# Two transformer blocks on one core: re-ordering a finished instruction list so that TensorE stays with one kind of product

## The chip, the cores and the metric

One NeuronCore of a Trainium2 chip. The metric is the device time of one execution in microseconds (us); lower is better. TensorE is called PE here, VectorE DVE, ScalarE ACT, GpSimd POOL; SP issues the DMAs.

## The reference

Both blocks work on 256 tokens of width 1024, in fp32, and each has two layers.

```python
def first_block(x, c, ...):                      # twice
    shift1, scale1, gate1, shift2, scale2, gate2 = split(silu(c) @ w_ada[l] + b_ada[l], 6)
    hdn = modulate(rmsnorm(x, norm1_g[l]), shift1, scale1)
    q_lat, c_kv, k_pe, sb_qkv, mb_qkv, gates = split(hdn @ w_in[l])     # 1024 -> 7200
    o_mla = causal_softmax_attention(...)        # latents of 768 and 256, normed, then w_uq, w_ukv
    o_sb  = stick_breaking_attention(...)
    o_mb  = moba_attention(...)
    g_a, g_b, g_c = split(sigmoid(gates), 3)
    merged = g_a*(o_mla @ w_o_mla[l]) + g_b*(o_sb @ w_o_sb[l]) + g_c*(o_mb @ w_o_moba[l])
    x = x + gate1 * (merged @ w_out[l])
    hdn = modulate(rmsnorm(x, norm2_g[l]), shift2, scale2)
    x = x + gate2 * (square(relu(hdn @ w_ff1[l])) @ w_ff2[l])           # 1024 -> 4096 -> 1024

def second_block(x, c, ctx, c_ctx, ...):         # _layer twice, the context only in the first
    h, hc = normed and modulated x and context
    parts = split(h @ w_in)                      # the context's parts likewise
    o_att = silu(z) * attention(rope(q), [k_context; rope(k)], [v_context; v])
    o_f = silu(z) * (real(fftn(u)) @ w_fourier)
    o_c, o_p = convolution and pooling branches
    x = x + gate * (concat(o_f, o_att, o_c, o_p) @ w_out)
```

## The kernel before

The program is not written in the order in which it runs. `record` (line 493) describes the whole computation once, as a list of operations for five queues: PE, DVE, ACT, POOL and SP. `Recorder.add` (line 230) finds for each operation which others it depends on. `Scheduler.run` (line 425) then simulates the list with a table of costs and sets a start time for each operation; `emit` (line 434) sorts the list by that time (line 451) and writes each instruction at line 454, which is why every row of the trace says L454. On the chip every engine goes through its own queue in that order and waits at its head until what the instruction needs is there. So the order decides who waits.

The scheduler is a list scheduler. `forward` (line 341) takes the operation with the smallest priority whose predecessors are placed and whose buffers are free, and puts it into the first gap of its engine that is long enough. `backward` (line 406) works out how late each could start, and that becomes the priority of the next of five passes, less an offset from the table `LEAD` (line 1792), which has numbers for each part of the model, with or without an engine. Buffers come from pools (`SLOTS`, `CAPS`, lines 1788, 1789): at most 24 split weight tiles and 8 raw ones at once. Two things are not in the scheduler's costs: that PE may take longer after a change of the kind of product, and which PE work could fill a wait.

A weight tile (`wload`, line 596) is brought by a DMA (`raw`), rounded to fp32r on ACT (`whi`), and the remainder is made on DVE (`wlo`). A large product (`mm3`, line 523) is three fp32r matmuls: high by high, high by low, low by high. On PE there are three kinds of instructions: 6920 fp32r products, 538 transposes of 128x128 blocks, and 412 plain fp32 products (scores, probabilities by values, row sums).

The names that the rows use: `g`, `gc`, `ff`, `f`, `cb`, `qkvp`, `ufp` are PSUM tiles of the large products; `nT_ql`, `nT_kvl`, `nT_x`, `nT_c` are transposes of normed rows (`norm_T`, line 782: the latents for queries and keys in the first block, x and the context in the second; the number behind the name is layer and token half); `xn_...` are those rows, made on DVE; `s_ml`, `s_l` are score tiles, `p_...` their softmax (DVE and ACT), `pT_...` its transposes on PE, and `pv` the product with the values; `gh`, `yt`, `of` are the three steps of the Fourier branch, with copies between them.

```python
    with tc.manual_schedule():
        for op in sorted(rec.ops, key=lambda o: (o.start, o.idx)):
```

Of the kernel before, what the change touches and what calls it, by code (L numbers as in the profile page):

```python
# [14 lines left out]
F32 = mybir.dt.float32  # L15
# [3 lines left out]
ALU = mybir.AluOpType  # L19
# [11 lines left out]
PSUM_CLASSES = ("mm", "tr")  # L31
# [112 lines left out]

class Op:
    __slots__ = ("idx", "eng", "fn", "args", "kw", "cost", "preds", "succs", "bufs", "start", "end", "inst", "lead",
                 "calls")

    def __init__(self, idx, eng, fn, args, kw):
        self.idx, self.eng, self.fn, self.args, self.kw = idx, eng, fn, args, kw  # L150
# [17 lines left out]
class Recorder:  # L168
# [61 lines left out]
    def add(self, eng, fn, args, kw):  # L230
        if self.group:
            op = self.group[0]
        else:
            op = Op(len(self.ops), eng, fn, args, kw)
            op.lead = 0.0 if eng == "sync" else sum(
                LEAD.get(q, 0.0) for q in (self.part, self.stage, f"{self.stage}/{eng}"))
            self.ops.append(op)
# [83 lines left out]
class Scheduler:  # L321
# [84 lines left out]
    def backward(self):  # L406
# [15 lines left out]
            late[op.idx] = total - r - op.cost  # L422
        return late

    def run(self, passes):

        prio = list(range(len(self.ops)))
        for i in range(passes):
            if i > 0:
                prio = [t - op.lead for t, op in zip(self.backward(), self.ops)]  # L430
            self.forward(prio)


def emit(tc, ctx, rec):
    nc = tc.nc
    sb = ctx.enter_context(tc.tile_pool(name="sb", bufs=1))
    ps = ctx.enter_context(tc.tile_pool(name="ps", bufs=1, space=bass.MemoryType.PSUM))
    dr = ctx.enter_context(tc.tile_pool(name="dr", bufs=1, space=bass.MemoryType.DRAM))

    def val(x):  # L440
        if not isinstance(x, View):
            return x
        b = x.buf
        if b.real is None:
            pool = ps if b.cls in PSUM_CLASSES else dr if b.cls == "dram" else sb
            tag = b.name if b.slot is None else f"{b.cls}_{b.slot}"
            b.real = pool.tile(list(b.shape), b.dtype, tag=tag, name=b.name)
        return x.resolve()

    with tc.manual_schedule():  # L450
        for op in sorted(rec.ops, key=lambda o: (o.start, o.idx)):
            op.inst = []
            for fn, args, kw in op.calls:
                op.inst.append(getattr(getattr(nc, op.eng), fn)(*[val(x) for x in args],  # L454
                                                                 **{k: val(x) for k, x in kw.items()}))
# [37 lines left out]
def record(nc, a, out):  # L493
# [570 lines left out]
    def lead_first(g, act, banks):  # L1064
# [85 lines left out]
        first_weights.extend(last)  # L1150
        rate[0] = RATE

# [629 lines left out]
    for l in range(L):  # L1782
# [5 lines left out]
SLOTS = {"s4": 40, "s2": 11, "sm": 40, "mm": 4, "tr": 4}  # L1788
CAPS = {"w": 24, "r": 8}
PASSES = 5  # L1790
RATE = 0.4386
LEAD = {"None/sync": -6220.0, "None/tensor": -670.0, "None/vector": -290.0, "ada/sync": 8040.0, "att mb0": -60.0,
# [16 lines left out]
        "lead": 3119.0, "lead weights": 2070.0, "mb": -1510.0, "ml": -12100.0, "norm": 2550.0, "out mb0": -2320.0,  # L1809
# [22 lines left out]


@with_exitstack
def kernel(ctx: ExitStack, tc: tile.TileContext, a: dict, out: bass.AP):
    rec = Recorder()
    record(rec, a, out)
    Scheduler(rec, SLOTS, CAPS).run(PASSES)
    emit(tc, ctx, rec)
# [33 lines left out]
```

## Time and profile before

| what | value |
|---|---|
| median of 3 runs | 1278.47 us (1277.05 to 1279.66) |
| the profiled execution's own time | 1279.97 us |
| its span in the trace | 1278.2 us |
| PE busy | 1255.5 us, 98% |
| weight loads busy (beside PE) | 1112.8 us, 87% |
| DVE busy | 1043.1 us, 82% |
| ACT busy | 726.0 us, 57% |
| POOL busy | 85.2 us, 7% |
| DMA queue of the data | 62.9% of 16 engines' span |

The sums are made against the profiled execution: its span is 1278.2 us, and its own time is 1.8 us longer. Matmuls are pipelined, so a row's own duration on PE (0.39 us for one of 512 columns) overlaps the next one; the distance between the starts of two rows is what a product costs in a queue that never waits. A row with x4 is four equal instructions in succession.

### The profile page before, as it was taken

The page shows a single profiled execution, that of the slowest core. Times are in us where ns is not written, and L with a number is a line of the kernel's source. Part 1 is how long each engine was busy: PE and PEld are TensorE (multiplying, and loading weights), DVE is VectorE, ACT ScalarE, POOL GpSimd, SP SyncE. Part 2 cuts the span into 40 slices and gives each one's busy share as a digit, 9 for nine tenths or more (in the row PEclk, how much of TensorE's full clock was granted, in tenths as well). Part 3 has the DMA queues.
Part 4 walks back from the last instruction along what each step waited for, and adds up shares of the span by engine and source line. Part 5 has one row for each costly group of instructions (what it writes and reads, how often), then busy time and mean ns, then how long its engine had stood idle before and what let it go on. Part 6 is the DMA issues. An engine that isn't in the chain of part 4 may idle for free.

```text
span 1278.2 us, 22019 instructions
## 1 busy us (share of the span) xinstructions
PE 1255.5 (98%) x8282; PEld 1112.8 (87%) x8282; DVE 1043.1 (82%) x1707; ACT 726.0 (57%) x1247; POOL 85.2 (7%) x112
## 2 busy tenths in 40 slices
PE   6999999999999999999999999999999999999998
PEld 4899989998898989999889988899888777787997
DVE  4989989986876668798888879988878769958885
ACT  6597767554654546667576555555655353426561
POOL 1000000210000000000001200000002021100310
PEclk9999999999999999999999999999999999999999
DMA  8967665865997758576666766788652416716530
GB/s 295 367 236 240 210 224 202 280 199 191 315 300 275 253 165 276 182 246 200 233 205 198 266 231 228 269 275 279 210 190 79 156 31 215 238 34 213 175 119 33
DMA packets 164336, 272.68 MB, mean 213 GB/s; under 512 B 26411, under 2 KB 57343, under 8 KB 164230
## 3 DMA queue, kind: packets, MB, share of 16 engines
q1 hardware_dynamic: 164230, 271.28, 62.9%
q8 instruction: 65, 1.06, 0.3%
q14 instruction: 41, 0.34, 0.1%
HBM read 270.11 MB, written 1.13 MB: 212 GB/s over the span
## 4 chain that ended last, share of the span: by engine, by line
PE 88%; DMA 4%; DVE 3%; issue 2%; ACT 1%; SPq 1%; POOL 0%; ACTq 0%; POOLq 0%
PE gc L454 17%; PE g L454 16%; PE f L454 14%; PE ff L454 13%; PE cb L454 11%; PE qkvp L454 3%; DMA wraw_l<-lead_w 2%; PE ufp L454 1%; DMA araw_l<-lead_ada 1%; PE rs L454 1%; PE end L454 1%; DMA raw<-w_in 1%; PE pv L454 1%; PE s_l L454 1%; PE pT_l L454 1%
## 5 line engine op out<-in xcount | busy, mean ns | idle before, releaser
L454 DVE TENSOR_TENSOR wlo<-raw,whi 128x1024 fp32r<-128x1024 f32 (+2 forms) x354 | 407.8, 1184 | 57.5 <-ACT whi L454 32.6
L454 ACT CAST whi<-raw 128x1024 fp32r<-128x1024 f32 (+3 forms) x354 | 349.6, 1014 | 170.3 <-PE ff L454 43.2
L454 DVE SCALAR_TENSOR_TENSOR acc<-araw,cT,acc 128x1024 f32<-128x1024 f32 x147 | 191.9, 1330 | 1.3 <-DMA araw<-w_mod 0.6
L454 PE MATMUL gc<-hT1h,whi 128*128 128x256 f32 x256 | 73.9, 289 | 0.0
L454 PE MATMUL gc<-hT1h,wlo 128*128 128x256 f32 x256 | 71.8, 281 | 0.0
L454 PE MATMUL gc<-hT1l,whi 128*128 128x256 f32 x256 | 71.6, 280 | 0.0
L454 PE MATMUL f<-fT1h,whi 128*128 128x256 f32 x192 | 54.2, 282 | 0.0
L454 PE MATMUL f<-fT0h,whi 128*128 128x256 f32 x192 | 53.9, 281 | 0.0
L454 PE MATMUL f<-fT1h,wlo 128*128 128x256 f32 x192 | 53.9, 281 | 0.0
L454 PE MATMUL f<-fT1l,whi 128*128 128x256 f32 x192 | 53.9, 281 | 0.0
L454 PE MATMUL f<-fT0l,whi 128*128 128x256 f32 x192 | 53.8, 280 | 0.0
L454 PE MATMUL f<-fT0h,wlo 128*128 128x256 f32 x192 | 53.8, 280 | 0.0
L454 PE MATMUL cb<-h20h,whi 128*128 128x512 f32 x128 | 53.2, 416 | 0.0
L454 PE MATMUL gc<-hT0h,whi 128*128 128x256 f32 x176 | 51.5, 293 | 0.0
L454 PE MATMUL cb<-h20h,wlo 128*128 128x512 f32 x128 | 50.5, 394 | 0.0
L454 PE MATMUL cb<-h20l,whi 128*128 128x512 f32 x128 | 50.4, 394 | 0.0
L454 PEld LDWEIGHTS gc<-hT1h,whi 128*128 128x128 f32 x256 | 48.3, 189 | 1.8 <-issue 1.1
L454 PE MATMUL gc<-hT0l,whi 128*128 128x256 f32 x176 | 49.4, 281 | 0.0
L454 PE MATMUL gc<-hT0h,wlo 128*128 128x256 f32 x176 | 49.3, 280 | 0.0
L454 PEld LDWEIGHTS gc<-hT1l,whi 128*128 128x128 f32 x256 | 48.2, 188 | 0.6
L454 PEld LDWEIGHTS gc<-hT1h,wlo 128*128 128x128 f32 x256 | 48.2, 188 | 0.0
L454 PE MATMUL g<-whi,hT1h 128*128 128x512 f32 (+1 forms) x112 | 42.6, 380 | 0.0
(651 smaller groups left out, 3826.0 us busy)
## 6 DMA issues: line engine op xcount, KB each, us to landing
raw<-w_ff SPq DMA_DIRECT2D x128, 512.0 KB
raw<-w_in SPq DMA_DIRECT2D x126, 512.0 KB
araw<-w_ada SPq DMA_DIRECT2D x96, 256.0 KB
araw<-w_ada SPq DMA_DIRECT2D x32, 512.0 KB
raw<-w_out SPq DMA_DIRECT2D x32, 512.0 KB
araw<-w_mod SPq DMA_DIRECT2D x64, 256.0 KB
raw<-w_in SPq DMA_DIRECT2D x24, 352.0 KB
araw_l<-lead_ada SPq DMA_DIRECT2D x32, 256.0 KB
```

The costliest lines, as they stand in the source:

```text
L454: op.inst.append(getattr(getattr(nc, op.eng), fn)(*[val(x) for x in args], **{k: val(x) for k, x in kw.items()}))
```

## The change

No instruction is added or removed, but for one more loading of an ACT table (10 in place of 9). Two things are new. First, a function `settle` is called at the end of `run`. It takes the schedule that the five passes left, keeps the order on DVE, ACT, POOL and SP and the buffers, and runs the whole list once more in order of time with other costs: `span` for the durations, `HAND` for the time from one engine to the next, and `TURN` for what PE is to pay when one kind of product follows another (kind 0 fp32r, 1 transposes, 2 and 3 fp32 with a wide or a narrow result). Whenever PE's next operation is not ready, or is a large product while PE is at another kind, it looks up to 4 us (`LOOK`) further down the list and takes a ready one, of the same sort if there is one, for at most 1.5 us of work in succession (`MOST`). The order it finds is what `emit` writes. Second, the table `LEAD` has new numbers, so the schedule that `settle` starts from is another.

```diff
+    HAND = {"tensor": 200.0, "vector": 150.0, "scalar": 150.0, "gpsimd": 100.0}
+    TURN = ((0.0, 0.0, 60.0, 92.0), (84.0, 0.0, 0.0, 92.0), (188.0, 0.0, 0.0, 100.0), (239.0, 135.0, 135.0, 0.0))
...
+    def settle(self, look, most):
...
+            q = queue["tensor"]
+            while taken[q[head["tensor"]]]:
+                head["tensor"] += 1
+            h = head["tensor"]
+            first, now = q[h], free["tensor"]
+            late = left[first] > 0 or ready(first) > now + 100.0
+            i = first
+            if last is not None and (late or last[0] and not form[first][0]) and ahead < most:
+                other = None
+                for j in range(h + 1, len(q)):
+                    c = q[j]
+                    if ops[c].start > ops[first].start + look:
+                        break
+                    if taken[c] or left[c] or ready(c) > now + 60.0:
+                        continue
+                    if bool(form[c][0]) == bool(last[0]):
+                        other = c
+                        break
+                    if late and other is None:
+                        other = c
+                if other is not None:
+                    i = other
...
+            ahead = 0.0 if i == first else ahead + span[i]
+            t = max(now, ready(i))
...
+            elif form[i][0] != last[0]:
+                t += self.TURN[last[0]][form[i][0]]
...
     def run(self, passes):
...
+        self.settle(LOOK, MOST)
...
-        for op in sorted(rec.ops, key=lambda o: (o.start, o.idx)):
+        for op in sorted(rec.ops, key=lambda o: o.seq):
...
+LOOK, MOST = 4000.0, 1500.0
...
-LEAD = {"None/sync": -6220.0, "None/tensor": -670.0, "None/vector": -290.0, "ada/sync": 8040.0, "att mb0": -60.0,
+LEAD = {"None/scalar": 2080.0, "None/sync": -5820.0, "None/tensor": -670.0, "None/vector": -290.0,
```

Counted over PE's whole queue, there are 164 stretches of transposes before and 98 after, 36 stretches of wide fp32 products and then 28, and 42 of narrow ones in both. The places where the order differs that matter below are three; all are on PE.

**At the boundary of the second block's two layers**, where the context's normed rows `xn_c` are transposed. `qkvp` is the projection of x to queries, keys and values of layer 1. Before, six of its products stand ahead of `nT_c12`:

```order
L454 MATMUL qkvp10_12938<-whi182_0_12591,h21h0_12809 128x512
L454 MATMUL qkvp10_12938<-wlo182_0_12636,h21h0_12809 128x512
L454 MATMUL qkvp10_12938<-whi182_0_12591,h21l0_12828 128x512
L454 MATMUL qkvp10_12938<-whi182_0_12591,h21h0_12809 128x512
L454 MATMUL qkvp10_12938<-wlo182_0_12636,h21h0_12809 128x512
L454 MATMUL qkvp10_12938<-whi182_0_12591,h21l0_12828 128x512
L454 MATMUL nT_c120_12960<-ct_79,xn_c12_12953 128x128 x4
L454 MATMUL nT_c124_12965<-ct_79,xn_c12_12953 128x128 x4
L454 MATMUL qkvp10_12938<-whi182_2_12604,h21h1_12817 128x512
```

Now twelve stand there (ten of them shown); the six more are products that came behind the transposes before:

```order
L634 MATMUL qkvp10_12961<-whi182_0_12566,h21l0_12821 128x512
L634 MATMUL qkvp10_12961<-whi182_0_12566,h21h0_12810 128x512
L634 MATMUL qkvp10_12961<-wlo182_0_12618,h21h0_12810 128x512
L634 MATMUL qkvp10_12961<-whi182_0_12566,h21l0_12821 128x512
L634 MATMUL qkvp10_12961<-whi182_2_12614,h21h1_12814 128x512
L634 MATMUL qkvp10_12961<-wlo182_2_12620,h21h1_12814 128x512
L634 MATMUL qkvp10_12961<-whi182_2_12614,h21l1_12825 128x512
L634 MATMUL qkvp10_12961<-whi182_2_12614,h21h1_12814 128x512
L634 MATMUL qkvp10_12961<-wlo182_2_12620,h21h1_12814 128x512
L634 MATMUL qkvp10_12961<-whi182_2_12614,h21l1_12825 128x512
L634 MATMUL nT_c120_12974<-ct_79,xn_c12_12956 128x128 x4
L634 MATMUL nT_c124_12985<-ct_79,xn_c12_12956 128x128 x4
```

In the same way there are 12 products ahead of the second half's `nT_c` in place of 3 that had nothing of it to wait for, and three more `g` products ahead of `nT_x11`.

**In the first layer, at the transposes of the key latents** `nT_kvl01`. `g8` is the up-projection of the query latents and `s_sb` a score of the stick-breaking attention. Before, the transposes follow those of the query latents at once:

```order
L454 MATMUL g8_00_1216<-whi8_2_946,laT0l0_1207 128x384
L454 MATMUL nT_ql010_1249<-ct_79,xn_ql01_1242 128x128 x4
L454 MATMUL nT_ql014_1256<-ct_79,xn_ql01_1242 128x128 x2
L454 MATMUL nT_kvl010_1261<-ct_79,xn_kvl01_1225 128x128 x2
L454 MATMUL g8_00_1216<-whi9_0_1005,laT0h1_1205 128x384
L454 MATMUL g8_00_1216<-wlo9_0_1066,laT0h1_1205 128x384
L454 MATMUL g8_00_1216<-whi9_0_1005,laT0l1_1220 128x384
```

Now six `g8` products, which stood behind them or ahead of `nT_ql01`, and a score stand between:

```order
L634 MATMUL nT_ql010_1246<-ct_79,xn_ql01_1207 128x128 x4
L634 MATMUL nT_ql014_1257<-ct_79,xn_ql01_1207 128x128 x2
L634 MATMUL g8_00_1236<-whi8_2_956,laT0h0_1178 128x384
L634 MATMUL g8_00_1236<-wlo8_2_961,laT0h0_1178 128x384
L634 MATMUL g8_00_1236<-whi8_2_956,laT0l0_1194 128x384
L634 MATMUL g8_00_1236<-whi9_0_1000,laT0h1_1192 128x384
L634 MATMUL g8_00_1236<-wlo9_0_1005,laT0h1_1192 128x384
L634 MATMUL g8_00_1236<-whi9_0_1000,laT0l1_1199 128x384
L634 MATMUL s_sb011_1274<-kssb01_805,qssb01_776 128x256
L634 MATMUL nT_kvl010_1276<-ct_79,xn_kvl01_1202 128x128 x2
L634 MATMUL s_sb011_1274<-k_low1_75,qssb01_776 128x256
```

**At the end of attention in the last layer**, where `pT_l1101`, transposes of softmaxed scores, are followed by the products with the values. `cb` is the product with the columns of the convolution and pooling branches. Before, three of its four transposes stand further up, each alone, and the last one here:

```order
L454 MATMUL cb1_1792_0_13872<-h21l3_12842,whi191_4_13667 128x256
L454 MATMUL cb1_1792_0_13872<-h21h3_12833,wlo191_4_13858 128x256
L454 MATMUL cb1_1792_1_13890<-h21h3_12833,whi191_4_13667 128x256
L454 MATMUL cb1_1792_1_13890<-h21l3_12842,whi191_4_13667 128x256
L454 MATMUL cb1_1792_1_13890<-h21h3_12833,wlo191_4_13858 128x256
L454 MATMUL pT_l1101_14070<-ct_79,p_l1101_14019 128x128
L454 MATMUL pv2101_14072<-pTs_l1001_13999,qkv10_13027 64x128
L454 MATMUL pv2101_14072<-pTs_l1011_14064,qkv10_13027 64x128
```

Now three groups of four stand together, and `pv` follows:

```order
L634 MATMUL cb1_1536_0_13950<-h21l1_12825,whi190_0_13412 128x256
L634 MATMUL cb1_1536_0_13950<-h21h1_12814,wlo190_0_13717 128x256
L634 MATMUL cb1_1536_1_13954<-h21h1_12814,whi190_0_13412 128x256
L634 MATMUL cb1_1536_1_13954<-h21l1_12825,whi190_0_13412 128x256
L634 MATMUL cb1_1536_1_13954<-h21h1_12814,wlo190_0_13717 128x256
L634 MATMUL pT_l1011_13976<-ct_79,p_l1011_13848 128x128 x4
L634 MATMUL pT_l1101_13993<-ct_79,p_l1101_13940 128x128 x4
L634 MATMUL pT_l1111_14000<-ct_79,p_l1111_13894 128x128 x4
L634 MATMUL pv2101_14015<-pTs_l1001_13929,qkv10_13064 64x128
```

Between the second score product of this softmax, `s_l1101`, and its transposes stand now 24 `cb` products and one group of transposes.

## Rows read from the trace of the kernel before

**Rows 1.** The page: busy time by engine; granted clock of PE in 40 slices, in tenths.

```profile
PE 1255.5 (98%) x8282; PEld 1112.8 (87%) x8282; DVE 1043.1 (82%) x1707; ACT 726.0 (57%) x1247; POOL 85.2 (7%) x112
...
PEclk9999999999999999999999999999999999999999
```

**Rows 2.** Windows: us, then PE, PEld, DVE, ACT, POOL busy, clock, DMA.

```profile
9.00:70.00 61.00, 56.37 (x380) 48.46 (x381) 48.63 (x99) 36.57 (x57) 0.56 (x1) 1.00 0.97 343
70.00:1000.00 930.00, 928.44 (x6273) 839.97 (x6272) 778.71 (x1188) 558.78 (x933) 42.60 (x52) 1.00 0.68 229
...
1170.00:1195.00 25.00, 25.00 (x199) 24.38 (x198) 23.69 (x55) 14.28 (x25) 5.13 (x4) 1.00 0.62 200
```

**Rows 3.** Timeline of PE at a lone transpose (start us, duration us, instruction).

```profile
653.89 0.28 PE L454 MATMUL gc<-hT1h,wlo 128*128 128x256 f32 x1
654.02 0.27 PE L454 MATMUL pT_ml<-ct,p_ml 128*128 128x128 f32 x1
...
654.25 0.28 PE L454 MATMUL gc<-hT1l,whi 128*128 128x256 f32 x1
654.37 0.28 PE L454 MATMUL gc<-hT1h,wlo 128*128 128x256 f32 x1
```

**Rows 4.** Timeline of PE: plain fp32 scores; one product behind each is left out.

```profile
188.85 1.03 PE L454 MATMUL s_ml<-mkT,mqT 96*128 96x256 f32 x4
...
189.95 0.39 PE L454 MATMUL g<-wlo,hT0h 128*128 128x512 f32 x1
...
622.85 0.61 PE L454 MATMUL s_ml<-mkT,mqT 96*128 96x128 f32 x4
...
623.52 0.40 PE L454 MATMUL g<-wlo,hT1h 128*128 128x512 f32 x1
```

**Rows 5.** Timeline of PE between the second block's layers.

```profile
1151.23 1.06 PE L454 MATMUL nT_x<-ct,xn_x 128*128 128x128 f32 x8 [0.53 <-DVE xn_x L454]
...
1158.15 0.39 PE L454 MATMUL qkvp<-whi,h21l 128*128 128x512 f32 x1
1160.04 1.06 PE L454 MATMUL nT_c<-ct,xn_c 128*128 128x128 f32 x8 [1.50 <-DVE xn_c L454]
...
1161.17 0.40 PE L454 MATMUL qkvp<-wlo,h21h 128*128 128x512 f32 x1
...
1165.59 0.40 PE L454 MATMUL qkvp<-whi,h21l 128*128 128x512 f32 x1
1166.65 1.07 PE L454 MATMUL nT_c<-ct,xn_c 128*128 128x128 f32 x8 [0.66 <-ACT sq L454]
```

**Rows 6.** Timeline of PE before the key latents' transposes, first layer.

```profile
99.63 0.82 PE L454 MATMUL nT_ql<-ct,xn_ql 128*128 128x128 f32 x6
101.08 0.44 PE L454 MATMUL nT_kvl<-ct,xn_kvl 128*128 128x128 f32 x2 [0.63 <-ACT p_sb L454]
```

**Rows 7.** Timeline of PE in the Fourier branch, second block's first layer.

```profile
1012.72 1.03 PE L454 MATMUL gh<-late,uf 128*128 128x256 f32 x4
1013.97 0.68 PE L454 MATMUL yt<-gh011s,late 128*128 128x129 f32 x4 [0.22 <-DVE tl_yT L454]
1014.49 0.60 PE L454 MATMUL gh<-late,uf 128*128 128x256 f32 x2
1015.28 0.49 PE L454 MATMUL yt<-gh000s,late 128*128 128x129 f32 x2 [0.20 <-ACT gh000s L454]
```

**Rows 8.** Timeline of ACT: a table loading.

```profile
0.73 1.28 ACT L454 ACT_TABLE_LOAD   x1 [0.73 <-PEq L1864]
```

**Rows 9.** Timelines: layer 1, score `s_l1101` on PE, its probabilities on DVE.

```profile
1232.23 0.39 PE L454 MATMUL s_l<-kL,qT 128*128 128x512 f32 x1
...
1239.03 0.49 DVE L454 TENSOR_SCALAR p_l<-p_l,ru_l 128x512 f32<-128x512 f32 x1
```

**Rows 10.** Timelines: layer 0, score `s_l0111` on PE, its probabilities on DVE.

```profile
1026.66 0.63 PE L454 MATMUL s_l<-kL,qT 128*128 128x512 f32 x2
...
1032.47 0.48 DVE L454 TENSOR_SCALAR p_l<-p_l,ru_l 128x512 f32<-128x512 f32 x1
```

More of the change, by code (lines that the diff above doesn't have):

```diff
@@ L146 @@
     __slots__ = ("idx", "eng", "fn", "args", "kw", "cost", "preds", "succs", "bufs", "start", "end", "inst", "lead",
-                 "calls")
+                 "calls", "seq")
     def __init__(self, idx, eng, fn, args, kw):
@@ L423, in backward, with form @@
         return late
+    HAND = {"tensor": 200.0, "vector": 150.0, "scalar": 150.0, "gpsimd": 100.0}
+    SAME = {"vector": 150.0, "scalar": 150.0, "gpsimd": 100.0}
+    TURN = ((0.0, 0.0, 60.0, 92.0), (84.0, 0.0, 0.0, 92.0), (188.0, 0.0, 0.0, 100.0), (239.0, 135.0, 135.0, 0.0))
+    @staticmethod
+    def form(op):
+        fn, args, _ = op.calls[0]
+        up = lambda v: 32 if v <= 32 else 64 if v <= 64 else 128
+        shape = (up(args[1].shape[0]), up(args[0].shape[0]))
+        if fn == "transpose":
+            return 1, shape
+        if args[1].ap.dtype != F32:
+            return 0, shape
+        return (2 if shape[1] == 128 or shape[0] < shape[1] else 3), shape
@@ new lines, in span @@
+    @staticmethod
+    def span(op):
+        c = 0.0
+        for fn, a, k in op.calls:
+            out = k.get("out", a[0] if a else None)
+            n = out.free_size()
+            if op.eng == "tensor":
+                if fn == "transpose":
+                    c += 109.0
+                elif a[1].ap.dtype != F32:
+                    c += max(n * 0.445 + 4.0, 111.0)
+                else:
+                    m = out.shape[0]
+                    c += (max(n, 128) * 4 / 2.4 + 8.0) * (m / 128 if m in (32, 64) else 1.0)
+                continue
+            x = Recorder.cost(op.eng, fn, a, k, out)
+            if fn == "tensor_tensor_scan":
+                x = n * 2.09 + 69.0
+            if op.eng == "vector" and n >= 1024:
+                x += 25.0
+            if op.eng == "gpsimd" and fn == "tensor_tensor":
+                x = {1: 900.0, 2: 1050.0, 6: 1450.0}.get(n, x * 1.15) if k.get("op") == ALU.pow else x * 1.05
+            if op.eng == "scalar" and k.get("accum_out") is not None:
+                x += 10.0
+            c += x
+        return c
@@ new lines, in shares_port @@
+    @staticmethod
+    def shares_port(op):
+        if op.eng not in ("vector", "gpsimd"):
+            return False
+        if op.eng == "gpsimd":
+            return True
+        fn, a, k = op.calls[0]
+        views = [x for x in list(a) + list(k.values()) if isinstance(x, View) and x.free_size() > 1]
+        out = k.get("out", a[0] if a else None)
+        if any(v.buf.cls in PSUM_CLASSES for v in views):
+            return False
+        return len([v for v in views if v is not out]) >= 2 or fn in ("tensor_copy", "tensor_scalar", "memset")
@@ new lines, in settle, with ready, finish @@
+    def settle(self, look, most):
+        ops = self.ops
+        waits = [[(p, raw) for p, raw in op.preds.items()] for op in ops]
+        for x, y in self.edges:
+            waits[y.ops[0].idx].extend((q.idx, "buffer") for q in x.ops)
+        after = [[] for _ in ops]
+        left = [0] * len(ops)
+        for i, w in enumerate(waits):
+            left[i] = len(w)
+            for p, _ in w:
+                after[p].append(i)
+        span = [self.span(op) for op in ops]
+        form = [self.form(op) if op.eng == "tensor" else None for op in ops]
+        port = [self.shares_port(op) for op in ops]
+        queue = {e: [] for e in Recorder.ENGINES}
+        for op in sorted(ops, key=lambda o: (o.start, o.idx)):
+            queue[op.eng].append(op.idx)
+        head = {e: 0 for e in queue}
+        free = {e: 0.0 for e in queue}
+        issue, dma = 700.0, 0.0
+        start, end, seq = [0.0] * len(ops), [0.0] * len(ops), [0] * len(ops)
+        taken = [False] * len(ops)
+        busy = {"vector": [], "gpsimd": []}
+        done = 0
+        def ready(i):
+            eng, t = ops[i].eng, 0.0
+            for p, raw in waits[i]:
+                if raw is None:
+                    continue
+                e = ops[p].eng
+                if eng == "sync":
+                    t = max(t, end[p] + (100.0 if e == "sync" else self.HAND[e]))
+                elif e == eng:
+                    if e != "tensor" and raw is True:
+                        t = max(t, end[p] + self.SAME[e])
+                else:
+                    t = max(t, end[p] + (0.0 if e == "sync" else self.HAND[e]))
+            return t
+        def finish(i):
+            nonlocal done
+            taken[i], seq[i] = True, done
+            done += 1
+            for q in after[i]:
+                left[q] -= 1
+        last, ahead = None, 0.0
+        while done < len(ops):
+            pick = None
+            for e in queue:
+                if e != "tensor" and head[e] < len(queue[e]):
+                    i = queue[e][head[e]]
+                    if left[i] == 0 and (pick is None or (ops[i].start, i) < (ops[pick].start, pick)):
+                        pick = i
+            if pick is not None:
+                i, e = pick, ops[pick].eng
+                head[e] += 1
+                if e == "sync":
+                    t = max(issue, ready(i))
+                    issue = t + 450.0
+                    _, _, k = ops[i].calls[0]
+                    v = k["out"] if isinstance(k["out"], View) else k["in_"]
+                    dma = max(t + 1800.0, dma) + max(v.free_size() * v.shape[0] * 4 / 330.0, 100.0)
+                    start[i], end[i] = t, dma + 1300.0
+                else:
+                    t = max(free[e], ready(i))
+                    if port[i]:
+                        for s, f in reversed(busy["gpsimd" if e == "vector" else "vector"][-6:]):
+                            if s <= t < f:
+                                t = f
+                                break
+                        busy[e].append((t, t + span[i]))
+                    start[i] = t
+                    free[e] = end[i] = t + span[i]
+                finish(i)
+                continue
+            q = queue["tensor"]
[12 more added lines that the diff above has]
+                    if taken[c] or left[c] or ready(c) > now + 60.0:
+                        continue
+                    if bool(form[c][0]) == bool(last[0]):
+                        other = c
+                        break
+                    if late and other is None:
+                        other = c
+                if other is not None:
+                    i = other
+            if left[i]:
+                raise RuntimeError("no order")
+            ahead = 0.0 if i == first else ahead + span[i]
+            t = max(now, ready(i))
+            if last is None:
+                t += 100.0
+            elif form[i][0] != last[0]:
+                t += self.TURN[last[0]][form[i][0]]
+            elif form[i][1] != last[1]:
+                t += 100.0
+            last = form[i]
+            start[i] = t
+            free["tensor"] = end[i] = t + span[i]
+            finish(i)
+        for op in ops:
+            op.start, op.end, op.seq = start[op.idx], end[op.idx], seq[op.idx]
+        return max(end)
@@ L1790 @@
 PASSES = 5
+LOOK, MOST = 4000.0, 1500.0
 RATE = 0.4386
-LEAD = {"None/sync": -6220.0, "None/tensor": -670.0, "None/vector": -290.0, "ada/sync": 8040.0, "att mb0": -60.0,
[16 rows of a table removed]
-        "lead": 3119.0, "lead weights": 2070.0, "mb": -1510.0, "ml": -12100.0, "norm": 2550.0, "out mb0": -2320.0,
[22 rows of a table removed]
+LEAD = {"None/scalar": 2080.0, "None/sync": -5820.0, "None/tensor": -670.0, "None/vector": -290.0,
+        "ada/sync": 5250.0, "ada/tensor": -210.0, "att mb0/scalar": 290.0, "att mb0/tensor": 3900.0,
[40 rows of a table added]
 @with_exitstack
```

78 rows, old and new, of the table LEAD are left out of this document.

## The prediction

> **What bounds the kernel now.** I read the page's busy times first. [...] So two things can be saved: the 22.7 us in which PE is idle, and time that PE spends without need while it counts as busy, as after a change of the kind of product.
>
> Of the idle time, the first 9 us lie ahead of PE's first instruction, and from 9 to 70 us PE is idle for 61.00 - 56.37 = 4.63 us [rows 2]. There the kernel waits for its first weights, with the DMA engines 97% busy. SP issues its first seventy transfers in the same order after the change, so I take nothing for these. From 70 to 1000 us PE is idle for 930.00 - 928.44 = 1.56 us [rows 2]. What is left, about 7.5 us, lies behind 1000 us: at the boundary between the second block's layers, in its Fourier branch, in its attention, and in a tail of some 4 us. That is all that filling waits can win; the rest must come from the changes of kind.
>
> **What a change of kind costs.** The table `TURN` says 84 ns from a transpose to an fp32r product, 60 and 188 ns into and out of a wide fp32 one. Counting each succession in both queues by it, the turns cost 33.4 us before and 23.5 after: 9.8 us less, 6.1 of them from transposes. The trace gives another price. From 653.89 to 654.25 stand one product, one transpose and one product: 0.36 us [rows 3]. A product of 256 columns takes 0.12 (654.25 to 654.37), so the lone transpose takes 0.12. In a run of eight, 1160.04 to 1161.17 is 1.13 us with one product of 512 columns in it; nineteen of those take 0.233 each (1161.17 to 1165.59) [rows 5]. That leaves 0.90, or 0.112 for each transpose. A turn to a transpose and back costs at most 0.01 us. There are 66 stretches of transposes fewer: 0 to 0.7 us, and I take 0.3.
>
> Wide fp32 scores: four of 256 columns take 1.10 - 0.23 = 0.87 us up to the second product behind them, four of 128 columns 0.67 - 0.23 = 0.44 [rows 4]. Half the columns take half the time, so the fixed part is 2 x 0.44 - 0.87 = 0.01 us, and 8 stretches fewer save nothing. Narrow ones have 42 stretches in both orders: nothing.
>
> **What the moved work fills.**
> - Boundary. `nT_x11` has 0.53 us of idle time ahead of it [rows 5]; three more `g` products of 0.233 cover it: -0.5. `nT_c12` starts at 1160.04, 1.89 after the product before it, whose own 0.23 leaves 1.66; six more products are 1.40: -1.4. The second `nT_c` waits 1.06 - 0.23 = 0.83, with nine more products (2.1 us) ahead: -0.8. Together -2.7.
> - Key latents. 101.08 - 99.63 = 1.45, six transposes take 0.67, so 0.78 is wait [rows 6]. Six products of 384 columns, at 384/512 x 0.233 = 0.175, are 1.05: -0.8.
> - Fourier branch of layer 0. Four `gh` by 1.25 us up to `yt`, of which 0.87 is their own by the scores of the same size [rows 4]: 0.38 wait; two by 0.79 where 0.44 is their own: 0.35 [rows 7]. The change spreads these steps between large products: -0.7.
>
> The sum so far: -0.3 - 2.7 - 0.8 - 0.7 = **-4.5 us**.
>
> **What it may cost.** Where transposes are gathered, the probabilities of several heads must be there at once, and everything behind them on PE waits too (`pv`, then the products that need the concatenation). Two places have less cover than the row of before shows the softmax to take. `s_l1101` starts at 1232.23, and its probabilities are done at 1239.03 + 0.49 = 1239.52, 7.3 us later [rows 9]. The new order has the score's own 0.23 us, 24 `cb` products (2.8) and four transposes (0.45) between: 3.5 us, so up to 3.8 of wait. `s_l0111`, second of the pair at 1026.66, starts near 1026.9 and is answered at 1032.95, 6.1 later [rows 10]; the new order leaves 4.7 us of products between: up to 1.4. The bounds are 0 and 5.2 us. I take **+0.8**, nearer to nothing: before, nobody was in a hurry for these answers, DVE was busy with weight remainders meanwhile, and in the new order DVE has the step for `p_l1101` three places earlier in its queue.
>
> The one more ACT table takes 1.28 us [rows 8]. ACT is busy for 57% [rows 1] and its casts run ahead of PE: nothing; 1.28 if a softmax stands right behind it. POOL's pooling steps are moved a little, end well before their readers, and cost nothing. DVE's order hardly moves, but from 1170 to 1195 it is busy for 23.69 of 25 us [rows 2]: what PE gains at the boundary it may lose again there, because the remainders `wlo` come no earlier. That is in the rivals.
>
> **The sum**: -4.5 + 0.8 = -3.7. The profiled execution took 1279.97 us (span 1278.2), so it would take 1276.3; the median of the runs shown, 1278.47, lies 1.5 below it, and less 3.7 gives **1274.8 us**. A measurement of this kernel can tell about 0.2%, 2.6 us, from no change.
>
> **Rivals.**
> - *The turns are as dear as the table says* (faster). 9.8 us plus 4.3 of filled waits less 0.8 would give 1278.47 - 13.3 = 1265.2. Against it stand [rows 3 to 5]: the turns that it counts are not there.
> - *The new waits eat the gain* (no change). Some 4 us of the 5.2 come true, or a part of the boundary's 2.7 is given back: about 1278. For it: DVE is full behind the boundary [rows 2].
> - *DVE answers late in the last layers* (slower). Its place is the softmax of the second block, its price the upper bounds. DVE goes at its own pace from 1170 on, so the 2.7 come back as waits for `wlo`; the two gathered sets of transposes wait 3.8 and 1.4: 1278.47 - 4.5 + 2.7 + 3.8 + 1.4 = 1281.9. It decides at whether DVE and ACT answer `s_l1101` later than 3.5 us after it. For it: 7.3 in the row [rows 9]. Against: that answer had time.
> [...]
> - *The change does not do what it says*: the queue does have fewer turns and more work ahead of the waits named, so what can fail is their worth, which the cases above hold; no chance of its own.
>
> **How the numbers follow.** Forecast 0.53; turns as in the table 0.05; waits eat the gain 0.24; clock 0.03; DVE late 0.15. Faster by over 0.2% is 0.53 + 0.05 = 0.58, within 0.2% is 0.24 + 0.03 = 0.27, slower 0.15. The likeliest case's own range is 1272.5 to 1276: down by 0.8 if no new wait comes, 0.4 more from turns, and some 1 us of small idle gaps that I did not cost; up by another 1.2 of waits. The range for 8 in 10 runs from **1268.5**, between this and the first rival, to **1282.0**, where half of the slower case is still inside.
>
> **What would show it.** Right: lone transposes and those in runs still at 0.11 to 0.12 us; `nT_c12` with 0.3 us of wait in place of 1.66 and the second `nT_c` with none; `nT_kvl01` with none; PE busy within 1 us of 1255.5 and idle time down by about 4. Wrong: PE's busy time down by several us (then turns do cost); waits for `p_l` ahead of `pT_l1101` or `pT_l0111`, or for `whi` and `wlo` from 1165 to 1210, which together exceed 2 us; a clock below its level behind long runs; or the first 70 us changed by over 1 us, which I took as the same.

## The result and the profile after

The change made the kernel slower: 1285.82 us, median of 4 runs (1285.39 to 1288.8), beside 1278.09 for the kernel before, a ratio of 1.0064 (95% interval 1.0046 to 1.0083). Forecast were 1274.8 us and a range that ended at 1282.0.

From the page of the profiled execution (1288.8 us), busy times and PE's granted clock by slice:

```profile
PE 1258.3 (98%) x8282; PEld 1116.2 (87%) x8282; DVE 1042.6 (81%) x1707; ACT 723.9 (56%) x1248; POOL 88.6 (7%) x112
...
PEclk9999999999999999999999999999999899999999
```

PE is busy for 2.8 us more than before, and it has 28.7 us of idle time (its span of 1287.0 less 1258.3) in place of 22.7 [rows 1]. One slice shows a lower clock, 8 tenths, and there was none before. What PE waited for, in us in all, number of times, and the longest:

```profile
PE yt L634 <- ACT tl_yT L634: 6.1, 6, 4.0
...
PE pv L634 <- ACT py L634: 1.8, 1, 1.8
...
PE pT_l L634 <- DVE p_l L634: 0.6, 1, 0.6
```

The first line is the news: 6.1 us ahead of `yt`, the second step of the Fourier branch, where before there was 0.4 [rows 7]. Then 1.8 us ahead of a `pv` that did not wait at all before. On the timeline of PE:

```profile
1003.50 0.39 PE L634 MATMUL yt<-gh010s,late 128*128 128x129 f32 x2
1004.24 0.49 PE L634 MATMUL yt<-gh010s,late 128*128 128x127 f32 x2 [0.36 <-ACT tl_yT L634]
1004.57 0.39 PE L634 MATMUL yt<-gh011s,late 128*128 128x129 f32 x2
1005.31 0.49 PE L634 MATMUL yt<-gh011s,late 128*128 128x127 f32 x2 [0.36 <-ACT tl_yT L634]
...
1006.78 0.39 PE L634 MATMUL yt<-gh000s,late 128*128 128x129 f32 x2
1011.22 0.79 PE L634 MATMUL yt<-gh000s,late 128*128 128x127 f32 x2 [4.05 <-ACT tl_yT L634]
...
1012.30 0.99 PE L634 MATMUL cb<-h20h,whi 128*128 128x512 f32 x1
1013.09 0.63 PE L634 MATMUL cb<-h20l,whi 128*128 128x512 f32 x1
...
1016.45 0.39 PE L634 MATMUL s_l<-kT,qT 128*128 128x512 f32 x1
```

Each `yt` tile is made by two products, the first for 129 columns and the second for 127, each written as two equal instructions here. Between the two there is now a wait for ACT's copy `tl_yT` of the first half, 0.36 us where ACT is free and 4.05 us at 1006.78. Behind that the `cb` products stand 0.42 to 0.43 us apart for some 4 us, in place of 0.233. ACT at this place:

```profile
1005.84 0.37 ACT L634 COPY gh000s<-gh 128x256 f32<-128x256 f32 x1 [0.58 <-PE yt L634]
1006.98 0.65 ACT L634 CAST qT<-qT 128x256 fp32r<-128x256 f32 x2 [0.77 <-PE qT L634]
1009.95 1.04 ACT L634 CAST whi<-raw 128x1024 fp32r<-128x1024 f32 x1 [2.32 <-DVE wlo L634]
1010.90 0.26 ACT L634 COPY tl_yT<-yt 128x129 f32<-128x129 f32 x1
```

The copy that PE waits for needs nothing but the first product, done by 1007.2, but it stands in ACT's queue behind a cast of a weight tile, and that cast waits 2.32 us for DVE, whose timeline has three long steps on weights in succession, up to 1009.9:

```profile
1006.36 1.22 DVE L634 TENSOR_TENSOR wlo<-raw,whi 128x1024 fp32r<-128x1024 f32 x1
1007.50 1.28 DVE L634 SCALAR_TENSOR_TENSOR acc<-araw,cT,acc 128x1024 f32<-128x1024 f32 x1
1008.69 1.22 DVE L634 TENSOR_TENSOR wlo<-raw,whi 128x1024 fp32r<-128x1024 f32 x1
```

The places that the forecast named. PE at the layer boundary and at the key latents:

```profile
1162.27 1.07 PE L634 MATMUL nT_x<-ct,xn_x 128*128 128x128 f32 x8 [0.45 <-DVE xn_x L634]
...
1170.80 1.06 PE L634 MATMUL nT_c<-ct,xn_c 128*128 128x128 f32 x8 [0.51 <-DVE xn_c L634]
...
1177.40 1.06 PE L634 MATMUL nT_c<-ct,xn_c 128*128 128x128 f32 x8
...
99.85 0.82 PE L634 MATMUL nT_ql<-ct,xn_ql 128*128 128x128 f32 x6
...
101.68 0.39 PE L634 MATMUL s_sb<-kssb,qssb 128*128 128x256 f32 x1
101.90 0.38 PE L634 MATMUL nT_kvl<-ct,xn_kvl 128*128 128x128 f32 x2
```

Against [rows 5] the waits ahead of `nT_c` went from 1.50 to 0.51 us and from 0.66 to none, that ahead of `nT_x11` from 0.53 to 0.45 only, and `nT_kvl` no longer waits [rows 6].

The difference adds up roughly. The `yt` waits are 5.7 us more, the nine products from 1012.30 to 1016.45 take 4.15 where they would take 2.1, `pv` and `pT_l` wait 2.3 more, and the boundary and the key latents give back 1.7 and 0.6: 7.7 of the 8.8 us by which the spans differ. Of the rest, 0.8 lies at the start: PE's 400th instruction begins at 74.1 us in place of 73.3. In this execution the clock was also lower in the first 70 us, where before it was 1.00 [rows 2] (us, busy times of the five engines, then the granted clock, the third figure from the end):

```profile
9.00:70.00 61.00, 55.42 (x376) 47.34 (x377) 47.12 (x98) 35.53 (x54) 0.56 (x1) 0.94 0.99 345
```

The profile of e2 below, with the same order on PE, has 1.00 there. So this part belongs to the one execution that was profiled; it may be why that one took 3 us more than the median of its kernel, which no run settles.

### The profile page after: what moved, and what is told of

Same layout as the page of the kernel before. It is cut to its first block, busy times and chain, and to the rows that moved or that the text cites. A ratio compares the mean times of both kernels' runs of the same rounds, so it can differ in the third digit from the quotient of the medians.

```text
span 1287.0 us, 21981 instructions
## 1 busy us (share of the span) xinstructions
PE 1258.3 (98%) x8282; PEld 1116.2 (87%) x8282; DVE 1042.6 (81%) x1707; ACT 723.9 (56%) x1248; POOL 88.6 (7%) x112
## 4 chain that ended last, share of the span: by engine, by line
PE 89%; DMA 4%; DVE 3%; ACT 2%; issue 1%; SPq 1%; POOL 0%; DVEq 0%; ACTq 0%; POOLq 0%
PE gc L634 17%; PE g L634 16%; PE f L634 14%; PE ff L634 14%; PE cb L634 10%; DMA wraw_l<-lead_w 3%; PE qkvp L634 3%; PE ufp L634 1%; PE rs L634 1%; PE end L634 1%; PE s_ml L634 1%; PE pv L634 1%; PE s_l L634 1%; PE pT_l L634 1%; DVE acc L634 1%
## 5 line engine op out<-in xcount | busy, mean ns | idle before, releaser
L634 DVE TENSOR_TENSOR wlo<-raw,whi 128x1024 fp32r<-128x1024 f32 (+3 forms) x354 | 407.8, 1184 | 53.4 <-ACT whi L634 30.0
```

## The experiments

Why should the second product wait for the copy of the first half? No value passes from one to the other: the halves are different columns. `Recorder` sees that, and its list has no edge between them. But the runs show that the waits follow the order of writing as well, and whole tiles: with the second products written behind the copies of their tiles' first halves, PE waited for those copies six times in the change (0.36 to 4.05 us) and four times in e8 (1.4 us in all); with the list of the change written in order of time (e1) it did not. So it matters in which order the list is *written*, not only in which order each engine runs it. Before, it was written in order of start times, and the copy came behind the second product for four of the six `yt` tiles. `settle` numbers operations as it takes them, and it takes all that it can on DVE, ACT and POOL ahead of PE's next: for all six the copy is written ahead of the second product, though its start time is the later one. I call this **theory F**, false waits by the order of writing: false because no value is waited for. Whether the two could be at one tile at the same time, no run here tries. **Theory Q** puts the loss on ACT's queue: short copies behind casts that wait for DVE. **Theory O** puts it on the new offsets.

**e1: written in order of time.** Every engine's own order is that of the change; in the two traces PE, DVE, ACT and POOL have the same instructions in the same succession, name by name.

```diff
+        when, line, old = list(start), {}, [[] for _ in ops]
+        for x, y in self.edges:
+            for o in y.ops:
+                old[o.idx].extend(q.idx for q in x.ops)
+        for i in sorted(range(len(ops)), key=lambda i: seq[i]):
+            e = ops[i].eng
+            when[i] = max([when[i], line.get(e, 0.0)] + [when[p] for p in ops[i].preds] + [when[q] for q in old[i]])
+            line[e] = when[i]
+        rank = sorted(range(len(ops)), key=lambda i: (when[i], seq[i]))
+        for r, i in enumerate(rank):
+            seq[i] = r
```

> The change with every engine's own order kept, but the list written in the order of the start times that settle found, not in the order in which it took the operations. Theory F (false waits by the order of writing): each second yt product no longer waits for the copy of the first half, six waits of 0.36 to 4.05 us (6.1 in all) and the low clock behind the longest (eight products at 0.42 for 0.23, some 1.6 us) go: 1278 to 1281. Theory Q (ACT's queue: the copy stands behind a cast that waits for DVE, whatever the order of writing): the wait moves to the next reader, the of products, and the time stays at 1284 to 1286. Theory O (the new offsets): 1284 to 1286 as well.

Measured: 1277.7 us (1275.65 to 1280.57), ratio to before 0.9993 (0.9982 to 1.0004). The waits are gone; the four instructions of a tile now stand together on PE:

```profile
1000.14 0.61 PE L645 MATMUL yt<-gh010s,late 128*128 128x129 f32 x4
1000.59 0.61 PE L645 MATMUL yt<-gh011s,late 128*128 128x129 f32 x4
```

8.1 us for the order of writing alone. (The kernel before stood at 1278.92 us beside e1 to e4 and at 1278.09 beside the change, so a difference across these can be off by about 1 us.) The wait did not move to `of`, as Q would have it for this edit, and O by itself does not explain the loss.

**e2: the copy ahead of the cast.** On ACT, in the order of the change, `whi172_0` is put behind the copy of `yt000`.

```diff
+        seq[named["scalar", "whi172_0", "raw172_0"]] = seq[named["scalar", "tl_yT0", "yt000"]] + 0.5
```

> The change with one cast on ACT (whi172_0) put behind the copy of yt000 that stood behind it; order of writing as in the change. Theory F and theory Q alike: the wait of 4.05 us ahead of the second yt000 product falls to 0.4 and the clock stays up behind it: 1280 to 1282.5; the five waits of 0.36 to 0.6 stay. Theory O: within 1 us of the change, 1285 to 1287.

Measured: 1280.19 us (1279.28 to 1283.99), ratio 1.0012 (1.0002 to 1.0021). The waits of PE for these copies fell from 6.1 to 2.7 us, the longest 0.7, and the products of 512 columns behind it stand 0.23 us apart:

```profile
PE yt L640 <- ACT tl_yT L640: 2.7, 6, 0.7
```

So F and Q work together: the wait by order of writing alone is worth 0.4 to 0.7 us each time, and 4 us only where the copy stands behind a cast that waits for DVE. With the low clock behind it, this one place cost 5.6 of the 8.1 us.

**e3 and e4: settle and offsets apart.** e3 has `settle` with the `LEAD` of before; e4 has the new `LEAD` and no `settle`.

```diff
-        self.settle(LOOK, MOST)
...
-        for op in sorted(rec.ops, key=lambda o: o.seq):
+        for op in sorted(rec.ops, key=lambda o: (o.start, o.idx)):
```

> settle as in the change, but on the offsets of before. Theory F: settle writes the copies ahead of the second yt products here too, 2 to 6 us of waits against 0.8 before, less the waits that it fills: 1277 to 1283, slower than before. Theory O (the new offsets are what costs): 1273 to 1276, faster than before.

> The new offsets without settle, written in order of start times as before. Theory F: no second yt product waits for long: 1276 to 1281. Theory O: 1284 to 1288, as slow as the change. Theory Q: above 1282, since the cast stands ahead of the copy by the offsets.

Measured: e3 1283.21 us, ratio 1.0035 (1.0023 to 1.0047); e4 1284.27, ratio 1.0043 (1.0026 to 1.0060). e3 is as F says, slower on the old offsets too, though 0.2 us above F's range. Its largest wait has the same pattern on other engines. PE waits 3.76 us ahead of `pv_ml` for a copy on ACT, and ACT's and DVE's timelines show why:

```profile
656.68 0.58 ACT L634 CAST ksmb<-tt_mb 64x512 fp32r<-64x512 f32 x1 [4.73 <-DVE k_low L634]
657.28 0.59 ACT L634 COPY pTs_ml<-pT_ml 128x512 f32<-128x512 f32 x1
...
651.25 4.62 DVE L634 TENSOR_TENSOR wlo<-raw,whi 128x1024 fp32r<-128x1024 f32 x4
655.91 0.68 DVE L634 TENSOR_TENSOR k_low<-tt_mb,ksmb 64x512 fp32r<-64x512 f32 x1
```

The cast to `ksmb` waits 4.73 us for a DVE step that reads another part of the same tile, and that step stands behind four weight steps. e4 did not come out as F said. The new offsets on their own are 5.4 us slower than before, which O had foretold; `settle`, written in order of time, wins 6.6 back (e1). In the trace of e4 no second `yt` product waits; its largest new wait is again one for ACT's `py`, ahead of the `pv` that e6 treats:

```profile
PE pv L633 <- ACT py L633: 2.5, 1, 2.5
```

Behind it, from 1073.8 to 1080.8 us, the granted clock was 0.54, and the products stood 0.43 us apart in place of 0.233; over the whole execution the clock was 0.996, and 0.999 to 1.000 in the other three runs of e4. So most of what the new offsets lose in this profile is the order on ACT, as Q has it, though at another place than Q named. The profiled execution took 1287.22 us, 3 above the median of its four runs.

**e5: settle on the old offsets, written in order of time** (e3 with the edit of e1).

> The settle of the change on the offsets of before, written in order of start times. Theory F (false waits by the order of writing): against the same settle written in its own order (1283.2) the five yt waits (1.8 us) and the wait of 3.8 us ahead of pv_ml, behind a cast to ksmb that waits for a DVE step reading another part of the same tile, go: 1276.5 to 1279. Were these waits not due to the order of writing: 1282 to 1284.

Measured: 1278.0 us (1277.04 to 1279.71), ratio 0.9998 (0.9988 to 1.0007): 5.2 us for the order of writing on these offsets, with the 3.8 us ahead of `pv_ml` gone. With either table the time is that of the kernel before.

**e6: one more copy ahead of its cast.** e1, and on ACT a cast for the concatenation (`cat0h1`) put behind the two `py` instructions that empty the tiles of the pooling product.

```diff
+        seq[named["scalar", "cat0h1", "ct03_256"]] = seq[named["scalar", "py01", "pl01"]] + 0.5
```

> The change written in order of start times (1277.7), and on ACT one cast (cat0h1 from ct03) put behind the two readings of the pooling product (py). Theory Q (ACT's queue: short readings that PE waits for stand behind a cast that waits for DVE): the wait of 1.8 us ahead of pv in layer 0 and the slower products behind it go, 1274 to 1276.5. If DVE is what holds this place (the values' addition is late in any case), the wait goes to another reader: 1277 to 1278.5.

Measured: 1275.7 us (1274.79 to 1276.49), ratio 0.9977 (0.9966 to 0.9988). It beats both kernels, that of before by 0.2%. The cast and the two readings on ACT, in the change:

```profile
1080.40 0.30 ACT L634 CAST cat0h<-ct 128x128 fp32r<-128x128 f32 x1 [4.62 <-DVE ct L634]
1080.61 1.26 ACT L634 ACTIVATE py<-pl,vt 128x512 f32<-128x512 f32 x2
```

PE's timeline at this `pv`, of e1:

```profile
1067.67 0.40 PE L645 MATMUL cb<-h20h,wlo 128*128 128x512 f32 x1
1069.89 0.66 PE L645 MATMUL pv<-pTs_l,qkv 128*64 128x128 f32 x8 [1.83 <-ACT py L645]
```

and of e6, where it follows the products at once:

```profile
1068.53 0.66 PE L651 MATMUL pv<-pTs_l,qkv 128*64 128x128 f32 x8
```

Here the wait is a true one: `pv` is put into the PSUM tile that `py` reads. Only ACT's order made it long.

**e7 and e9: without regard to kinds.** In e7 (e1) and e9 (e6) `settle` takes a later operation only when the next is not ready, of any kind, and `TURN` is all zero; 138 stretches of transposes in place of 98.

```diff
-            if last is not None and (late or last[0] and not form[first][0]) and ahead < most:
+            if last is not None and late and ahead < most:
...
-                    if bool(form[c][0]) == bool(last[0]):
+                    if late:
```

> The change written in order of start times, but settle takes a later PE operation only when the next one is not ready, whatever its kind, and counts no price for turns: 138 stretches of transposes in place of 98. If a turn costs what the trace showed (0.01 us): 1276.7 to 1278.7, the same as with the grouping. If it costs what the table says (84 ns out of transposes, 60 and 188 about wide fp32): 3.4 us and more slower, above 1281.

> As the version with time order and py first (1275.7, PE busy 1252.4 us), but settle takes a later PE operation only when the next is not ready and regards no kind: 138 stretches of transposes in place of 98, some wide fp32 stretches more. The wait ahead of pv is gone in both, so what is left between them is the worth of the grouping. If turns cost what the lone transpose showed (0.01 us): 1275 to 1276.5. If the 2.3 us by which PE's busy time fell with the grouping are real time: 1277 to 1279. By the table: 1280 and more.

Measured: e7 1278.22 us, ratio 0.9992 (0.9983 to 1.0002); e9 1277.22 (1276.08 to 1278.74), ratio 0.9989 (0.9980 to 0.9998). e7 waits 0.7 us less ahead of `pv` than e1, so e9 beside e6 is the cleaner pair: 1.5 us by the medians, with intervals that overlap. PE's busy time, of e9 and then of e6:

```profile
PE 1253.9 (98%) x8282; PEld 1111.6 (87%) x8282; DVE 1042.1 (82%) x1707; ACT 725.2 (57%) x1248; POOL 88.7 (7%) x112
```

```profile
PE 1252.4 (98%) x8282; PEld 1112.1 (87%) x8282; DVE 1042.2 (82%) x1707; ACT 723.9 (57%) x1248; POOL 88.5 (7%) x112
```

The same 1.5 us; but e7, with the order of e9 on PE, has 1255.5, so busy times alone would not carry it. The table's price would be 3.4 us for the forty stretches of transposes alone.

**e8: the kernel before, with the copies written early.** The opposite test: nothing is changed but that each copy of a first half is written ahead of the product of the second half.

```diff
+            v = op.calls[0][1][0] if op.eng == "tensor" else None
+            if v is not None and v.buf.name in copies and v.buf.ops[1] is op:
+                c = copies.pop(v.buf.name)
+                if c not in out:
+                    out.append(c)
```

> The kernel before, every engine's order kept, but the ACT copies of the first halves of yt are written ahead of the PE products of the second halves, as the change writes them. Nothing else differs. Theory F: four more waits of 0.36 us and more on PE, since ACT's queue is short of work there none of 4 us: 1279.5 to 1282 beside 1278.5 for before. Without theory F: no difference.

Measured: 1280.29 us (1278.93 to 1282.26), ratio 1.0010 (1.0000 to 1.0019), and the waits are there, three of them in the first layer, at 0.36 us each; the first two:

```profile
1011.05 0.42 PE L466 MATMUL yt<-gh010s,late 128*128 128x129 f32 x2
1011.83 0.49 PE L466 MATMUL yt<-gh010s,late 128*128 128x127 f32 x2 [0.36 <-ACT tl_yT L466]
...
1013.02 0.49 PE L466 MATMUL yt<-gh011s,late 128*128 128x129 f32 x2
1013.87 0.49 PE L466 MATMUL yt<-gh011s,late 128*128 128x127 f32 x2 [0.36 <-ACT tl_yT L466]
```

That is 1.4 us slower than the 1278.85 of before in the same session, at the edge of what the interval can tell. Writing the same orders otherwise is enough to make the waits.

## Why the prediction was wrong

**The step that failed** is the item on the Fourier branch, "The change spreads these steps between large products: -0.7", and with it the bounds of what the change may cost, "0 and 5.2 us", which held answers of the softmax alone. I compared the order on each engine, and took a wait to follow from the data and the buffers. That the new sort key also changes in which order instructions of *different* engines are written, and that waits come from that, I did not weigh, though the line with the key is in the diff. In place of -0.7 there came +5.7 us of waits and 2 us of low clock. With the key mended and nothing else changed (e1) no `yt` product waits, and the kernel stands at 1277.7. The 0.7 was also read too large: the rows show 0.22 and 0.20 us of idle time there [rows 7].

**The boundary** (-2.7): mechanism right, size too large. It gave 1.7 in the trace. The three `g` products ahead of `nT_x11` stand ahead of the first half's `nT_x` as well. Between the two there are 33 products, as before; DVE's steps for the second half follow those for the first, so `xn_x` came later too, and 0.45 us of wait stays. And three of the six products more ahead of `nT_c12` only replace these `g` products, which stood between `nT_x11` and `nT_c12`: 30 products are there now and 27 were before. So the cover grew by 0.7 us and not by 1.4, and 0.51 stays. The forecast counted the same three products twice. For the second `nT_c`, with 24 products ahead of it in place of 21, 0.7 was enough.

**Key latents** (-0.8): right; the 0.63 us of idle time [rows 6] is gone.

**The turns** (-0.3): perhaps too small. e9 beside e6 gives 1.5 us for 40 of the 66 stretches, where the trace's price is at most 0.4 and the table's 3.4. That it is the turns is not shown. From start to start, a stretch of transposes between large products costs 0.006 us in e9 and 0.007 in e6 (medians of 112 and 63 stretches) above 0.109 for each transpose and the products' usual distance, so the price of [rows 3] stands. From its 400th instruction on PE is busy for 1195.9 us before, with 164 stretches, 1197.0 in e9 with 138, and 1195.5 in e6 with 98: more turns do not go with more time. What e6 wins over e9 stays open.

**The first 70 us** (taken as the same): PE's 400th instruction begins at 73.3 us before, at 74.1 in the change, and at 70.5 to 72.1 in e1, e2, e6, e7 and e9. e1 and e2, with the same order on PE, are 1.6 us apart, so what the change is worth there is not shown; but it was one of the forecast's own signs of being wrong, and a part of what the later profiles win lies there.

**The new waits** (+0.8, at most 5.2): neither of the two places waited. `s_l1101` is answered in time:

```profile
1240.03 0.40 PE L634 MATMUL s_l<-kL,qT 128*128 128x512 f32 x1
...
1243.22 1.47 PE L634 MATMUL pT_l<-ct,p_l 128*128 128x128 f32 x12
```

From the score to its transposes are 3.2 us, with no wait; the 7.3 of [rows 9] was the time of an answer that nobody wanted sooner. So the slower rival came true in its sign and not by its mechanism: DVE answered late, but a weight cast on ACT, not a softmax. The 1.8 us ahead of `pv` is a new wait that I had not listed, and so is one of 0.56 ahead of another `pT_l`, in layer 0; e6 shows that the first was the order on ACT.

**The clock.** The forecast gave 0.03 to a clock lowered by long runs of transposes, and counted that in the 0.27 for a time within 0.2%. No run shows such an effect. Here are windows of the change: before, in and behind the run of twelve at 1243.22:

```profile
1240.00:1243.20 3.20, 3.20 (x26) 2.91 (x25) 2.54 (x8) 2.79 (x8) 0.00 (x0) 1.00 0.42 153
1243.20:1244.70 1.50, 1.50 (x16) 1.33 (x16) 0.84 (x2) 1.41 (x3) 0.00 (x0) 1.00 0.09 34
1244.70:1249.00 4.30, 4.30 (x53) 4.13 (x54) 4.30 (x8) 2.39 (x5) 0.00 (x0) 1.00 0.00 0
```

It is 1.00 throughout. The longest runs, of fourteen and sixteen, lie between 580 and 980 us, where the clock is 1.00 as well. In the change, what stood ahead of a clock of 0.50 was idle time:

```profile
1001.00:1006.80 5.80, 5.08 (x29) 4.14 (x28) 2.92 (x7) 1.51 (x5) 0.00 (x0) 1.00 0.57 190
1006.80:1011.20 4.40, 0.37 (x4) 0.17 (x2) 4.40 (x5) 1.86 (x4) 0.00 (x0) 0.81 0.71 226
1011.20:1016.40 5.20, 5.18 (x13) 4.23 (x14) 1.59 (x3) 0.00 (x0) 0.00 (x0) 0.50 0.62 212
1016.40:1022.00 5.60, 5.24 (x23) 3.52 (x22) 1.88 (x5) 1.13 (x3) 0.00 (x0) 1.00 0.01 3
```

In 4.4 us PE was busy for 0.37. For the next 5.2 us the granted clock was 0.50, and then 1.00 again.

**The sum, once more.** With both repairs (e6) the kernel takes 1275.7 us, 0.9 above the 1274.8 that the forecast named for the work that was moved. That is luck: the boundary gave 1.0 less than forecast, and what made up for it is not shown: it may lie in the first 70 us, which were taken as the same, and in the 1.5 us between e9 and e6, of which 0.3 was priced. (In the first rival the waits filled come to 4.2 by the forecast's own terms, not 4.3.)

## What to carry to other kernels

Where waits are set by whole tiles, as here, the order in which a program is written is a part of its schedule: a sort key that kept every engine's order still made one engine wait for another (8.1 us between the change and e1), so compare the waits of the instructions, not only their places. A wait of 0.36 us became one of 4.05 where the copy waited for stood behind a cast that waited 2.32 itself; put short copies that free PSUM or feed PE ahead of casts that wait for another engine (5.6 us in e2, 2.0 in e6). When a change to a scheduler loses, undo its bookkeeping before its idea: here the numbering cost 8 us. The idea without it is no clear gain (e1 and e5 stand at the time of before); the 3 us of e6 hold the 2 us of one more cast moved on ACT.

## What the hardware showed that I had not expected

A wait of 4.05 us cost PE half as much again: the nine products behind it took 4.15 us in place of 2.1. In e1 a wait of 1.83 us ahead of `pv` was followed by a granted clock of 0.57 for four us:

```profile
1067.60:1069.90 2.30, 0.47 (x5) 0.04 (x3) 2.30 (x4) 0.95 (x3) 0.00 (x0) 1.00 0.06 9
1069.90:1073.90 4.00, 4.00 (x28) 2.27 (x29) 4.00 (x6) 0.52 (x1) 0.00 (x0) 0.57 0.59 171
```

In the change the same `pv` waited 1.78 us, and the products behind it kept 0.233 us of distance, at a clock of 1.00. So a wait of 1.8 us was followed by a lower clock in e1 and by none in the change; behind the 2.46 us ahead of the same `pv` in e4 it was 0.54 for 7 us.
